# In-projection duals of a gated hybrid block: six accumulators in turning pairs, q stored whole, short conv in PSUM

## The chip, the cores and the metric

One core of a Trainium2 chip. The metric is the device time of one launch in microseconds (us), the median of several runs. TensorE (PE) multiplies, VectorE (DVE) does two-input elementwise work, ScalarE (ACT) copies and evaluates activations, GpSimd (POOL) does elementwise work on SBUF, and SyncE (SP) issues most of the loads. PE writes only into PSUM, which has eight banks of 128 x 512 float32. Each engine works through its own instructions in a fixed order; an instruction that waits holds all behind it on that engine.

## The reference

One trunk layer over 1024 positions and 1024 channels, in float32. The part that matters here is the combined input projection and what follows each of its columns:

```python
proj = jnp.einsum('bsd,de->bse', h, w_in[l])
b_s, c_s, v_s, v_c, gl_c, gate_br = jnp.split(proj, SPLITS[:-1], axis=-1)

y_a = b_s * causal_dwconv(c_s * v_s, conv_short_w[l])        # width 3
y_a = jnp.einsum('bsc,cd->bsd', y_a, w_short_out[l])

u = v_c * jax.nn.sigmoid(gl_c)
u = causal_dwconv(u, conv_conf_w[l]) + conv_conf_b[l]         # width 31
u = jax.nn.silu(layer_norm(u, conf_ln_g[l], conf_ln_b[l]))
y_b = jnp.einsum('bsc,cd->bsd', u, w_conf_out[l])

g_a, g_b = jnp.split(jax.nn.sigmoid(gate_br), 2, axis=-1)
mix = jnp.einsum('bsd,de->bse', g_a * y_a + g_b * y_b, w_o[l])
```

Ahead of it stand an adaptive RMSNorm and its modulation; behind it a gated feed-forward network and a last norm.

## The kernel before

Channels lie on the 128 partitions, so a block of 128 channels by 1024 positions is one tile, and `halves` are its two halves of 512 positions. Each float32 operand of a matmul is split into a high and a low part (`split_w` for weights, lines 201 to 211; `split` for data), and each product is three matmuls: high by high, high by low, low by high (`mm3`, lines 285, 286 and 288). For a weight, ACT casts the high part `wh` (line 207), then POOL or DVE subtracts it from `raw` for the low part `wl` (line 208).

After a lead of seven column blocks and one more, the other 48 column blocks of the projection are worked off as twelve **duals** (here dual 0 to dual 11, in the order of `PAIRS`, two pairs in each). A dual computes a 2 x 2 block product with seven products instead of eight. The names of the products are M1 to M7 and their order is `PRODUCTS = "1265734"`: M1, M2, M6, M5, M7, M3, M4. Each has two halves, p = 0 and 1, one for each pair of the dual, and a half is 12 matmuls of 512 columns. Before M6 POOL makes the sums of weight blocks (lines 230 to 232), and before M3 one more (line 234). A unit of weights is prepared two products ahead (`next_w`, `AHEAD`), from three buffers each of `wh` and `wl` and five of `raw`; the four loads of the next dual are asked for at M3.

Each half of a product accumulates in a bank: M1, M6, M7 and M4 one after another in x, M2 in y, M5 and M3 in z. `win_evac` takes the values out after each product: c11 = M1 + M2, c12 = M1 + M6 + M5 + M3, c22 = M1 + M6 + M7 + M5 and c21 = -(M1 + M6 + M7 + M4), the signs being folded into what follows. ACT copies x after M1 (line 579) and after M6, and z after M5 (line 594), into SBUF; `plus` (line 547) adds a bank to such a copy. What a pair is, its kind says:

- `p` (channels of c_s and v_s): their product (lines 587 and 608), then `short_conv` (ACT line 538, DVE line 540, over all 1024 positions in SBUF).
- `q` (two blocks of b_s): times the short conv `sc` of two blocks (lines 589, 600, 611), then `q_store` splits the result: an ACT cast and a POOL subtraction for each half (lines 531 and 532) into a `qs` tile of high and low, stored from SP (line 534). In the last dual `q_load` brings high and low back, four transfers a block.
- `u` (v_c and gl_c): the gated product (lines 585 and 606) into `u`.
- `g` (two gate blocks): sigmoids, stored to DRAM by ACT.

The tiles of p, sc, u, sig and qs all come from one pool `uc` of eight. The width-31 conv (`conv`) is DVE work between all this: for each u tile two differences and 46 taps (line 649) of 512 columns, whose accumulators stand in the two banks left, `ps2`. A tap is ordered behind an instruction of the list `reads`, which holds the DVE additions of M2, M7 and M3; `CONV_READS = 66` spreads the taps over the first 66 of 72. ACT finishes a block of conv with two activations with the bias (line 662), and POOL adds it to `tot` (line 669). After the duals comes `ya` (the short branch's output projection), which needs all of q split.

Of the kernel before, what the change touches and what calls it, by code (L numbers as in the profile page):

```python
# [39 lines left out]
P = 128  # L40
# [35 lines left out]
PAIRS = [  # L76
# [4 lines left out]
]  # L81


CONV_READS = 66

NORM_AT = 1
LAG = 2  # L90
# [19 lines left out]
def block_kernel(ctx: ExitStack, tc: tile.TileContext, x0, xT, c, vecs, ada, w_first, w_plain, w_duals,  # L110
# [66 lines left out]
    def col(base, k):  # L177
        return vec[:, base + k : base + k + 1]
# [234 lines left out]
    def uc_tile(name, n=T + CK - 1, dt=F32):  # L413
        return ucp.tile([P, T + CK - 1], dt, tag="uc", name=name)[:, :n]
# [111 lines left out]

    def q_store(j):

        for h in range(2):
            s = uc_tile("qs", T, F32R)  # L530
            nc.scalar.copy(s[:, :H], sc[j][:, halves[h]])
            nc.gpsimd.tensor_tensor(s[:, H:], sc[j][:, halves[h]], f32(s[:, :H]), ALU.subtract)
            q_dram[j, h] = dram.tile([P, T], F32, name=f"q{j}{h}")
            nc.sync.dma_start(q_dram[j, h], f32(s))

    def short_conv(j, p):
        sc[j] = uc_tile(f"sc{j}", T)
        nc.scalar.activation(sc[j], p[:, :T], AF.Copy, scale=col(V_SW, j))
        for s in range(1, SK):
            nc.vector.scalar_tensor_tensor(  # L540
                out=sc[j], in0=p[:, s : s + T], scalar=col(V_SW + s * KC, j), in1=sc[j], op0=ALU.mult, op1=ALU.add
            )

    reads = []

    def plus(out, ps, b):
        reads.append(nc.vector.tensor_tensor(out, ps, b, ALU.add).ins)

    def minus_times(out, a, b):

        nc.vector.scalar_tensor_tensor(out=out, in0=a, scalar=-1.0, in1=b, op0=ALU.mult, op1=ALU.mult)

    def win_evac(pairs):

        st = [{} for _ in pairs]

        def start(e, kind, j):
            if kind == "u":
                u.append(u_tile(j))
                e["b"] = [u[j][:, CK - 1 + h * H : CK - 1 + (h + 1) * H] for h in range(2)]  # L560
            elif kind == "p":
                e["p"] = uc_tile(f"p{j}", T + SK - 1)
                nc.vector.memset(e["p"][:, : SK - 1], 0.0)
                e["b"] = [e["p"][:, SK - 1 + h * H : SK - 1 + (h + 1) * H] for h in range(2)]
            elif kind == "g":
                e["t"] = [uc_tile("sig", T) for _ in range(2)]
                e["b"], e["c"] = ([t[:, s] for s in halves] for t in e["t"])

        def evac(i, m, ps):
            kind, j, *rest = pairs[i]  # L570
            e = st[i]
            if m == "1":
                start(e, kind, j)
                if kind == "q":
                    e["b"] = [g_tile("m")]
            if m == "6" and kind == "q":
                e["b"].append(g_tile("v"))
            if m in "16":
                nc.scalar.copy(e["b"][m == "6"], ps)
            elif m in "23":  # L580
                h = m == "3"
                b = e["b"][h]
                plus(b, ps, b)
                if kind == "u" and h:
                    nc.vector.tensor_tensor(b, b, e["z"], ALU.mult)
                elif kind == "p" and h:
                    minus_times(b, e["z"], b)
                elif kind == "q":
                    nc.vector.tensor_tensor(sc[j][:, halves[h]], b, sc[j][:, halves[h]], ALU.mult)
                elif kind == "g":  # L590
                    nc.scalar.activation(b, b, AF.Sigmoid)
            elif m == "5":
                e["z"] = e["c"][1] if kind == "g" else g_tile("z")
                nc.scalar.copy(e["z"], ps)
            elif m == "7":
                plus(e["z"], ps, e["z"])
                if kind in "ug":
                    nc.scalar.activation(e["z"], e["z"], AF.Sigmoid, scale=-1.0)
                elif kind == "q":
                    minus_times(sc[j + 1][:, halves[1]], e["z"], sc[j + 1][:, halves[1]])  # L600
            else:
                if kind in "ug":
                    sig = e["c"][0] if kind == "g" else g_tile("sig")
                    nc.scalar.activation(sig, ps, AF.Sigmoid, scale=-1.0)
                if kind == "u":
                    nc.vector.tensor_tensor(e["b"][0], e["b"][0], sig, ALU.mult)
                elif kind == "p":
                    minus_times(e["b"][0], ps, e["b"][0])
                    short_conv(j, e["p"])
                elif kind == "q":  # L610
                    minus_times(sc[j + 1][:, halves[0]], ps, sc[j + 1][:, halves[0]])
                    for i in range(2):
                        q_store(j + i)
                else:
                    for g, t in zip((j, *rest), e["t"]):
                        nc.scalar.dma_start(gate_dram[g], t)
        return evac

    qT = [[None, None] for _ in range(KC)]

    def q_load(j, h):
        qT[j][h] = t_pair(f"q{j}{h}")
        for t, s in zip(qT[j][h], halves):
            nc.sync.dma_start(f32(t), q_dram[j, h][:, s])
# [6 lines left out]
    NE = (T + CK - 1) // 2  # L631
    TAPS = CK // 2 * 3 + 2

    def conv(j):
        eo = u[j].rearrange("p (n two) -> p n two", two=2)
        ev, od = eo[:, :, 0], eo[:, :, 1]
        diff = diffp.tile([P, T + CK - 1], F32, tag="diff", name="diff")
        d, e = diff[:, :NE], diff[:, NE : 2 * NE - 1]
        with tc.issue_after(reads[j * CONV_READS // KC]):
            nc.vector.tensor_tensor(d, ev, od, ALU.subtract)  # L640
            nc.vector.tensor_tensor(e, ev[:, 1:], od[:, : NE - 1], ALU.subtract)
        a0, a1 = ps2_tile("c0"), ps2_tile("c1")
        n = 0

        def tap(out, src, s, wt, acc):
            nonlocal n
            n += 1
            with tc.issue_after(reads[(j * TAPS + n) * CONV_READS // (KC * TAPS)]):
                tap.ins = nc.vector.scalar_tensor_tensor(  # L649
                    out=out, in0=src[:, s : s + H], scalar=wt, in1=acc, op0=ALU.mult, op1=ALU.add  # L650
                ).ins

        nc.scalar.activation(a0, od[:, :H], AF.Copy, scale=wsum[:, j : j + 1])
        for s in range(1, CK // 2 + 1):
            last = s == CK // 2
            tap(a0, od, s, col(V_CW + 2 * s * KC, j) if last else wsum[:, s * KC + j : s * KC + j + 1], a0)
        for s in range(CK // 2):
            tap(a1, e, s, col(V_CW + (2 * s + 1) * KC, j), a1 if s else a0)
        for s in range(CK // 2 + 1):
            tap(a0, d, s, col(V_CW + 2 * s * KC, j), a0)  # L660
        for i, a in enumerate((a0, a1)):
            nc.scalar.activation(eo[:, : H, i], a, AF.Identity, bias=col(V_CB, j))
        nc.scalar.dma_start(cv_dram[j], u[j][:, :T])

    def add_conv(j):

        with tc.issue_after(pool_los[(j + 1) * CONV_READS * 7 // (6 * KC) + 5]):
            for h in range(2):
                nc.gpsimd.tensor_tensor(tot[h], tot[h], u[j][:, halves[h]], ALU.add)

# [34 lines left out]
        return [rstd_end(*r) for r in rs]  # L705

    n_duals = len(PAIRS) // 2
    for d in range(n_duals):
        banks, evac = {}, win_evac(PAIRS[2 * d : 2 * d + 2])
        for i, m in enumerate(PRODUCTS):  # L710
            product(banks, m, th[m], evac, y_tile=ps_tile)
            if d == n_duals - 1:
                for n in range(4 * i, min(4 * i + 4, 2 * KC)):
                    q_load(n // 2, n % 2)

    zs = {}

    def act_b(k, h):
# [467 lines left out]
```

## Time and profile before

| | us |
|---|---|
| median of three runs | 1514.88 |
| lowest, highest run | 1513.08, 1517.58 |
| span of the profiled execution | 1514.3 |
| first matmul of the duals, from the start of the span | 113.84 |
| first matmul of `ya` | 585.04 |
| PE busy | 1475.4 |
| DVE busy | 1173.1 |
| POOL busy | 580.2 |
| ACT busy | 613.6 |

A profile row of a group reads: line, engine, operation, output<-inputs, shapes, count | total busy us, mean ns of one | idle us of that engine right before them, with what ended it. A row of a timeline reads: start, duration, engine, line, operation, output<-inputs, shape, count, and in brackets how long the engine stood idle before it and what released it. A row of waits reads: who waited for whom, us in total, times, the longest. A busy PE is not PE at its peak, since matmuls overlap: in the profile one of 512 columns takes 0.39 us, while an undisturbed stretch starts one about every 0.227 us.

### The profile page before, as it was taken

To read this page: it belongs to the slowest core of one execution; us is meant where nothing else is said; L and a number is where in the kernel's file an instruction comes from. 1 tells how busy PE (TensorE), PEld (TensorE's weight loads), DVE (VectorE), ACT (ScalarE), POOL (GpSimd) and SP (SyncE) were. 2 spreads that over 40 slices of the span, in tenths; PEclk is the share of its full clock that TensorE was granted. 3 is DMA by queue.
4 is the path that set the end of the run, shared out by engine and by line. 5 is a ranking of instruction groups with operands and counts; after the bars stand their busy time and mean duration, and the time that the engine had idled before them with its cause. 6 is when DMAs were issued, how large, how long until landed. Compare 5 with 4: busy or idle time off the path is not lost.

```text
span 1514.3 us, 17807 instructions
## 1 busy us (share of the span) xinstructions
PE 1475.4 (97%) x6455; PEld 1203.2 (79%) x6455; DVE 1173.1 (77%) x1561; ACT 613.6 (41%) x875; POOL 580.2 (38%) x483
## 2 busy tenths in 40 slices
PE   6999999999998999999999989999999999999997
PEld 2788887877886888888788868888888888888887
DVE  7897898989998882857876798876666665767755
ACT  4654333333332442325335464444444443211235
POOL 0037788788768884320121101110000006444105
PEclk9999999999999999999999999999999999999999
DMA  9522224223222259655754527644444449997403
GB/s 347 206 64 84 84 71 139 70 98 111 98 84 85 69 192 408 239 197 173 249 193 155 167 89 231 209 153 153 153 153 153 153 150 363 348 330 241 152 28 112
DMA packets 87306, 255.64 MB, mean 169 GB/s; under 512 B 10033, under 2 KB 12209, under 8 KB 87218
## 3 DMA queue, kind: packets, MB, share of 16 engines
q1 hardware_dynamic: 46384, 146.30, 28.9%
q0 software_dynamic: 36944, 95.44, 19.0%
q10 hardware_dynamic: 3890, 12.78, 2.1%
q8 instruction: 50, 0.82, 0.2%
q14 instruction: 38, 0.31, 0.1%
HBM read 187.89 MB, written 66.58 MB: 168 GB/s over the span
## 4 chain that ended last, share of the span: by engine, by line
PE 78%; DVE 10%; POOL 7%; issue 3%; DMA 1%; ACT 1%; SPq 0%; POOLq 0%; ACTq 0%; DVEq 0%
PE x L288 10%; PE x L286 10%; PE x L285 10%; PE z L286 5%; PE z L285 5%; PE z L288 5%; DVE c L649 4%; PE y L288 3%; PE y L285 3%; PE y L286 3%; POOL wl L208 3%; PE ya L285 2%; PE mix L285 2%; PE mix L286 2%; PE ya L288 2%
## 5 line engine op out<-in xcount | busy, mean ns | idle before, releaser
L207 ACT CAST wh<-raw 128x1024 fp32r<-128x1024 f32 (+2 forms) x257 | 259.1, 1009 | 417.0 <-PE x L286 107.0
L208 POOL TENSOR_TENSOR wl<-raw,wh 128x1024 fp32r<-128x1024 f32 x92 | 237.0, 2584 | 87.6 <-ACT wh L207 81.1
L208 DVE TENSOR_TENSOR wl<-raw,wh 128x1024 fp32r<-128x1024 f32 (+2 forms) x165 | 188.1, 1141 | 50.8 <-ACT wh L207 48.4
L649 DVE SCALAR_TENSOR_TENSOR c<-diff,vec,c 128x512 f32<-128x512 f32 x248 | 182.2, 749 | 6.4 <-DMA q<-qs 2.6
L912 POOL DMA_DIRECT2D hid<-stage x71 | 37.9, 534 | 356.7 <-DVE stage L325 351.5
L285 PE MATMUL x<-th,wh 128*128 128x512 f32 x336 | 130.7, 389 | 0.0
L286 PE MATMUL x<-tl,wh 128*128 128x512 f32 x336 | 130.7, 389 | 0.0
L288 PE MATMUL x<-th,wl 128*128 128x512 f32 x336 | 130.7, 389 | 0.0
L649 DVE SCALAR_TENSOR_TENSOR c<-u,wsum,c 128x512 f32<-128x512 f32 x112 | 84.0, 750 | 2.0
L285 PE MATMUL x<-t2h,wh 128*128 128x512 f32 x184 | 73.6, 402 | 5.5 <-ACT wh L207 2.8
L288 PE MATMUL x<-t2h,wl 128*128 128x512 f32 x184 | 73.5, 400 | 4.5 <-POOL wl L208 4.2
L266 DVE CUSTOM_DVE_ANT_0 raw<-raw,cs,vec 128x1024 f32<-128x1024 f32 x24 | 36.9, 1541 | 48.9 <-DMA raw<-in_ada 39.7
L286 PE MATMUL x<-t2l,wh 128*128 128x512 f32 x184 | 73.4, 399 | 0.1
L286 PEld LDWEIGHTS x<-tl,wh 128*128 128x128 f32 x336 | 63.1, 188 | 13.2
L288 PEld LDWEIGHTS x<-th,wl 128*128 128x128 f32 x336 | 63.1, 188 | 13.1
L285 PEld LDWEIGHTS x<-th,wh 128*128 128x128 f32 x336 | 63.1, 188 | 13.0
L230 POOL TENSOR_TENSOR raw<-raw 128x1024 f32<-128x1024 f32 x12 | 29.2, 2437 | 99.1 <-DVE wl L208 95.3
L288 PE MATMUL z<-th,wl 128*128 128x512 f32 x168 | 65.5, 390 | 0.0
L285 PE MATMUL z<-th,wh 128*128 128x512 f32 x168 | 65.4, 389 | 0.0
L286 PE MATMUL z<-tl,wh 128*128 128x512 f32 x168 | 65.4, 389 | 0.0
L324 ACT CAST stage<-g 128x512 fp32r<-128x512 f32 x62 | 38.3, 621 | 54.6 <-DMA hid<-stage 26.8
L325 DVE TENSOR_TENSOR stage<-g,stage 128x512 fp32r<-128x512 f32 x62 | 42.4, 687 | 20.1 <-ACT stage L324 19.9
(802 smaller groups left out, 4076.5 us busy)
## 6 DMA issues: line engine op xcount, KB each, us to landing
hid<-stage POOLq DMA_DIRECT2D x71, 512.0 KB, 4.0
raw<-in_w_fi SPq DMA_DIRECT2D x50, 512.0 KB, 4.4
raw<-in_w_duals SPq DMA_DIRECT2D x48, 512.0 KB, 3.5
th<-hid POOLq DMA_DIRECT2D x71, 256.0 KB, 5.7
tl<-hid POOLq DMA_DIRECT2D x71, 256.0 KB, 5.8
ada<-in_ada SPq DMA_DIRECT2D x24, 512.0 KB, 6.4
raw<-in_ada SPq DMA_DIRECT2D x24, 512.0 KB, 4.5
raw<-in_w_fo SPq DMA_DIRECT2D x24, 384.0 KB, 5.8
```

The source lines that it names most:

```text
L207: nc.scalar.copy(wh, raw)
L208: lo = lo_engine.tensor_tensor(wl, raw, f32(wh), ALU.subtract)
L230: eng.tensor_tensor(a["s1"], a["21"], a["22"], ALU.add)
L266: nc.vector.tensor_tensor_reduce(out=raw, in0=raw, in1=cs, scale=1.0, scalar=col(V_ADA, b), op0=ALU.mult, op1=ALU.add, accum_out=modc(b),)
L285: nc.tensor.matmul(ps, wh, xh, start=first, stop=False, skip_group_check=again)
L286: nc.tensor.matmul(ps, wh, xl, start=False, stop=False, skip_group_check=again)
L288: mm3.ins = nc.tensor.matmul(ps, wl, xh, start=False, stop=last, skip_group_check=again).ins
L324: nc.scalar.copy(hi, src)
L325: nc.vector.tensor_tensor(lo, src, f32(hi), ALU.subtract)
L649: tap.ins = nc.vector.scalar_tensor_tensor(out=out, in0=src[:, s : s + H], scalar=wt, in1=acc, op0=ALU.mult, op1=ALU.add).ins
L912: nc.gpsimd.dma_start(hid_dram[key], s)
```

## The change

- Six PSUM tiles are taken once, as three pairs. Dual by dual they change places: the pair that was y becomes x, z becomes y, x becomes z.
- After M1, ACT copies x into y, and M2 accumulates on it there (its first matmul no longer starts a new sum). c11 then stands whole in y, and the addition after M2 goes; for `u` and `p` ACT copies y to SBUF, for `g` its sigmoid reads y, for `q` DVE multiplies from y.
- c12 is added up in z and c21 taken from x, and multiplies and sigmoids read these banks. The u sigmoid of c21 is written into x itself.
- The short conv accumulates in the two x banks by halves; its last tap writes `sc`.
- q is stored whole, one transfer a block, with no split. In the last dual, after its first four products, it is loaded whole, and ACT and DVE split it.
- `reads` holds the instructions after M7, M3 and M4, each with a place in units of a product; the taps are spread evenly over 11.2 duals by place.
- In `PAIRS`, u7 goes into dual 8 in place of p6, and dual 9 gets p6 and p7.

The core of the diff:

```diff
-    ("q", 4), ("p", 6), ("p", 7), ("u", 7), ("q", 6), ("g", ("a", 2), ("a", 3)),
+    ("q", 4), ("u", 7), ("p", 6), ("p", 7), ("q", 6), ("g", ("a", 2), ("a", 3)),
...
-CONV_READS = 66
+CONV_DUALS = 11.2
+AT_READS = {"7": 4.5, "3": 5.5, "4": 6.5}
...
     def q_store(j):
-        for h in range(2):
-            s = uc_tile("qs", T, F32R)
-            nc.scalar.copy(s[:, :H], sc[j][:, halves[h]])
-            nc.gpsimd.tensor_tensor(s[:, H:], sc[j][:, halves[h]], f32(s[:, :H]), ALU.subtract)
-            q_dram[j, h] = dram.tile([P, T], F32, name=f"q{j}{h}")
-            nc.sync.dma_start(q_dram[j, h], f32(s))
+        q_dram[j] = dram.tile([P, T], F32, name=f"q{j}")
+        nc.sync.dma_start(q_dram[j], sc[j])
+
+    def short_conv(j, p, banks):
+        sc[j] = uc_tile(f"sc{j}", T)
+        for h, bank in enumerate(banks):
+            nc.scalar.activation(bank, p[:, h * H : (h + 1) * H], AF.Copy, scale=col(V_SW, j))
+        for h, bank in enumerate(banks):
+            for s in range(1, SK):
+                nc.vector.scalar_tensor_tensor(
+                    out=sc[j][:, halves[h]] if s == SK - 1 else bank, in0=p[:, h * H + s : h * H + s + H],
+                    scalar=col(V_SW + s * KC, j), in1=bank, op0=ALU.mult, op1=ALU.add
+                )
...
+    def q_load(j):
+        t = uc_tile("q", T)
+        nc.sync.dma_start(t, q_dram[j])
+        for h in range(2):
+            qT[j][h] = split(t[:, halves[h]], hl_tile, f"q{j}{h}")
...
+    def win_dual(d, pairs, x, y, z):
...
+        def c22(p, e, kind, j, *more):
+            src = y[p] if kind == "q" else e["5"]
+            add = nc.vector.tensor_tensor(src, x[p], e["5"], ALU.add)
...
+        def c12(p, e, kind, j, *more):
+            add = nc.vector.tensor_tensor(z[p], z[p], e["6"], ALU.add)
...
+            if kind == "u":
+                return times(e["b"][1], z[p], e["z"])
...
+        def c21(p, e, kind, j, *more):
...
+            if kind == "u":
+                nc.scalar.activation(x[p], x[p], AF.Sigmoid, scale=-1.0)
+                return times(e["b"][0], x[p], e["b"][0])
...
+        banks = {"1": x, "6": x, "7": x, "4": x, "2": y, "5": z, "3": z}
+        for m in PRODUCTS:
+            w = next_w()
+            for p in range(2):
+                ps, e = banks[m][p], st[p]
+                for k in range(KH):
+                    c0 = (p * KH + k) * P
+                    mm3([ps], slice(c0, c0 + P), w, [th[m][k]], m in "15" and k == 0, k == KH - 1, m not in "15")
+                if m == "1":
+                    nc.scalar.copy(y[p], ps)
+                elif m in "65":
+                    e[m] = g_tile("v")
+                    nc.scalar.copy(e[m], ps)
+                else:
+                    done = {"2": c11, "7": c22, "3": c12, "4": c21}[m](p, e, *pairs[p])
+                    if done is not None:
+                        reads.append((7 * d + AT_READS[m] + 0.5 * p, done.ins))
+            if d == len(PAIRS) // 2 - 1 and m in "1265":
+                for j in range(2):
+                    q_load(2 * "1265".index(m) + j)
+        for e, (kind, j, *more) in zip(st, pairs):
+            if kind == "p":
+                short_conv(j, e["t"], x)
+            elif kind == "q":
+                for i in range(2):
+                    q_store(j + i)
...
+    def paced(n):
+        at = 7 * CONV_DUALS * n / (KC * TAPS)
+        return [ins for when, ins in reads if when <= max(at, reads[0][0])][-1]
...
+    banks = [[ps_tile(b) for _ in range(2)] for b in "xyz"]
     for d in range(n_duals):
-        banks, evac = {}, win_evac(PAIRS[2 * d : 2 * d + 2])
-        for i, m in enumerate(PRODUCTS):
-            product(banks, m, th[m], evac, y_tile=ps_tile)
+        win_dual(d, PAIRS[2 * d : 2 * d + 2], *banks)
+        banks.append(banks.pop(0))
```

More of the change, by code (lines that the diff above doesn't have):

```diff
@@ L527, in q_store @@
     def q_store(j):
-        for h in range(2):
-            s = uc_tile("qs", T, F32R)
-            nc.scalar.copy(s[:, :H], sc[j][:, halves[h]])
-            nc.gpsimd.tensor_tensor(s[:, H:], sc[j][:, halves[h]], f32(s[:, :H]), ALU.subtract)
-            q_dram[j, h] = dram.tile([P, T], F32, name=f"q{j}{h}")
-            nc.sync.dma_start(q_dram[j, h], f32(s))
[L536 to L553, printed above, removed]
-        st = [{} for _ in pairs]
-        def start(e, kind, j):
+        q_dram[j] = dram.tile([P, T], F32, name=f"q{j}")
[10 more added lines that the diff above has]
+                )
@@ new lines, in block_kernel, with minus_times, times, c11 @@
+    reads = []
+    def minus_times(out, a, b):
+        return nc.vector.scalar_tensor_tensor(out=out, in0=a, scalar=-1.0, in1=b, op0=ALU.mult, op1=ALU.mult)
+    def times(out, a, b):
+        return nc.vector.tensor_tensor(out, a, b, ALU.mult)
+    qT = [[None, None] for _ in range(KC)]
+    def q_load(j):
+        t = uc_tile("q", T)
+        nc.sync.dma_start(t, q_dram[j])
+        for h in range(2):
+            qT[j][h] = split(t[:, halves[h]], hl_tile, f"q{j}{h}")
+    def win_dual(d, pairs, x, y, z):
+        st = [{} for _ in pairs]
+        mul = any(kind == "q" for kind, *_ in pairs)
+        def c11(p, e, kind, j, *more):
+            if kind == "q":
+                times(sc[j][:, halves[0]], y[p], sc[j][:, halves[0]])
+                return
@@ L561, in start @@
             elif kind == "p":
[L562 to L565, printed above, removed]
+                e["t"] = uc_tile(f"p{j}", T + SK - 1)
+                nc.vector.memset(e["t"][:, : SK - 1], 0.0)
+                e["b"] = [e["t"][:, SK - 1 + h * H : SK - 1 + (h + 1) * H] for h in range(2)]
+            else:
@@ L566, in start @@
                 e["t"] = [uc_tile("sig", T) for _ in range(2)]
                 e["b"], e["c"] = ([t[:, s] for s in halves] for t in e["t"])
[L569 to L600, printed above, removed]
-            else:
[L602 to L613, printed above, removed]
-                else:
-                    for g, t in zip((j, *rest), e["t"]):
-                        nc.scalar.dma_start(gate_dram[g], t)
@@ L617, in win_evac @@
[L617 to L624, printed above, removed]
+            nc.scalar.activation(e["b"][0], y[p], AF.Sigmoid if kind == "g" else AF.Copy)
+        def c22(p, e, kind, j, *more):
+            src = y[p] if kind == "q" else e["5"]
+            add = nc.vector.tensor_tensor(src, x[p], e["5"], ALU.add)
+            if kind == "q":
+                return minus_times(sc[j + 1][:, halves[1]], src, sc[j + 1][:, halves[1]])
+            if kind == "p":
+                e["z"] = src
+            else:
+                e["z"] = e["c"][1] if kind == "g" else src
+                nc.scalar.activation(e["z"], src, AF.Sigmoid, scale=-1.0)
+            return add
@@ new lines, in c12 @@
+        def c12(p, e, kind, j, *more):
+            add = nc.vector.tensor_tensor(z[p], z[p], e["6"], ALU.add)
+            if kind == "q":
+                return times(sc[j][:, halves[1]], z[p], sc[j][:, halves[1]])
+            if kind == "u":
+                return times(e["b"][1], z[p], e["z"])
+            if kind == "p":
+                return minus_times(e["b"][1], z[p], e["z"])
+            nc.scalar.activation(e["b"][1], z[p], AF.Sigmoid)
+            return add
+        def c21(p, e, kind, j, *more):
+            if kind == "q":
+                return minus_times(sc[j + 1][:, halves[0]], x[p], sc[j + 1][:, halves[0]])
+            if kind == "p":
+                return minus_times(e["b"][0], x[p], e["b"][0])
+            if kind == "u":
+                nc.scalar.activation(x[p], x[p], AF.Sigmoid, scale=-1.0)
+                return times(e["b"][0], x[p], e["b"][0])
+            nc.scalar.activation(e["c"][0], x[p], AF.Sigmoid, scale=-1.0)
@@ L627, in block_kernel @@
+        for e, (kind, j, *more) in zip(st, pairs):
+            if kind == "p":
+                short_conv(j, e["t"], x)
+            elif kind == "q":
+                for i in range(2):
+                    q_store(j + i)
+            elif kind == "g":
+                for g, t in zip((j, *more), e["t"]):
+                    nc.scalar.dma_start(gate_dram[g], t)
     taps = vec[:, V_CW : V_CW + CK // 2 * 2 * KC].rearrange("p (j two k) -> p j two k", two=2, k=KC)
@@ L638, in conv @@
         d, e = diff[:, :NE], diff[:, NE : 2 * NE - 1]
-        with tc.issue_after(reads[j * CONV_READS // KC]):
+        with tc.issue_after(paced(j * TAPS)):
             nc.vector.tensor_tensor(d, ev, od, ALU.subtract)
@@ L647, in tap @@
             n += 1
-            with tc.issue_after(reads[(j * TAPS + n) * CONV_READS // (KC * TAPS)]):
+            with tc.issue_after(paced(j * TAPS + n)):
                 tap.ins = nc.vector.scalar_tensor_tensor(
@@ L665, in add_conv @@
     def add_conv(j):
-        with tc.issue_after(pool_los[(j + 1) * CONV_READS * 7 // (6 * KC) + 5]):
+        with tc.issue_after(pool_los[min(int(7 * CONV_DUALS * (j + 1) / KC) + 5, len(pool_los) - 1)]):
             for h in range(2):
```

3 lines of the change are left out of this document (removed).

## The prediction

> **What bounds the kernel now.** I began with the busy table and went straight to the stage that the change edits, the twelve duals, one window each.
>
> ```profile
> PE 1475.4 (97%) x6455; PEld 1203.2 (79%) x6455; DVE 1173.1 (77%) x1561; ACT 613.6 (41%) x875; POOL 580.2 (38%) x483
> ...
> 113.84:151.92 38.08, 38.08 (x169) 31.53 (x168) 29.46 (x39) 15.55 (x21) 28.39 (x15) 1.00 0.25 83
> 228.08:267.34 39.26, 38.88 (x170) 31.30 (x168) 33.70 (x53) 14.56 (x20) 33.70 (x18) 1.00 0.39 134
> 305.42:345.60 40.18, 38.71 (x170) 31.38 (x168) 36.41 (x44) 15.45 (x21) 36.23 (x16) 1.00 0.28 95
> 345.60:385.46 39.86, 38.41 (x169) 31.46 (x168) 37.96 (x55) 15.82 (x22) 34.88 (x17) 1.00 0.31 106
> 461.62:508.88 47.26, 41.66 (x169) 33.60 (x168) 37.90 (x54) 15.78 (x20) 40.61 (x18) 0.93 0.26 89
> 546.96:585.04 38.08, 38.08 (x169) 31.53 (x168) 17.44 (x25) 16.22 (x24) 25.09 (x13) 1.00 0.88 330
> 113.84:585.04 471.20, 462.30 (x2017) 379.99 (x2016) 412.44 (x530) 177.94 (x241) 376.87 (x165) 0.99 0.32 110
> ```
>
> Columns after the window: its length, then busy us (count) of PE, PEld, DVE, ACT, POOL, granted clock, DMA share, GB/s. A dual is 7 products x 2 halves x 12 matmuls = 168. Dual 0 shows it undisturbed: 38.08 us, so 5.44 a product and 2.72 a half. Twelve of them are 457.0 us; the stage takes 471.2. The change removes no matmul, so **all that it can win in this stage is 14.2 us**, and the windows say where it lies: dual 3 1.2, dual 5 2.1, dual 6 1.8, dual 9 9.2 (sum 14.3); the other eight are clean. DVE, busy 412 of 471 us, is no bound by itself. What the PE waited for in this stage:
>
> ```profile
> PE x L288 <- POOL wl L208: 7.4, 4, 2.8
> PE y L288 <- POOL wl L208: 1.2, 1, 1.2
> PE x L285 <- ACT u L579: 0.4, 1, 0.4
> ...
> 465.08 0.80 PE L288 MATMUL x<-h00h,wl 128*128 128x512 f32 x1 [2.84 <-POOL wl L208]
> 465.67 0.63 PE L285 MATMUL x<-h10h,wh 128*128 128x512 f32 x1
> 480.40 0.50 PE L288 MATMUL x<-t2h,wl 128*128 128x512 f32 x1 [2.76 <-POOL wl L208]
> ```
>
> It is the low half of a weight, made on POOL, five times. After the two longest the matmul takes 0.63 us, and dual 9 has clock 0.93: 7% of 47.26 is 3.3 us lost at half rate, 1.65 for each of the two. So 5.9 of waiting costs 9.2.
>
> Why is POOL late there? Its rows ahead of the late weights of duals 3, 6 and 9 (and ACT's row ahead of dual 9's first):
>
> ```profile
> 234.54 2.56 POOL L532 TENSOR_TENSOR qs<-sc,qs 128x512 fp32r<-128x512 f32 x2
> 237.06 2.40 POOL L208 TENSOR_TENSOR wl<-raw,wh 128x1024 fp32r<-128x1024 f32 x1
> ...
> 353.13 3.02 POOL L532 TENSOR_TENSOR qs<-sc,qs 128x512 fp32r<-128x512 f32 x2
> 356.11 4.75 POOL L208 TENSOR_TENSOR wl<-raw,wh 128x1024 fp32r<-128x1024 f32 x2
> ...
> 460.01 0.62 ACT L531 CAST qs<-sc 128x512 fp32r<-128x512 f32 x1 [6.98 <-DVE sc L589]
> 460.54 1.04 ACT L207 CAST wh<-raw 128x1024 fp32r<-128x1024 f32 x1
> ...
> 473.54 4.51 POOL L532 TENSOR_TENSOR qs<-sc,qs 128x512 fp32r<-128x512 f32 x2
> 478.00 4.71 POOL L208 TENSOR_TENSOR wl<-raw,wh 128x1024 fp32r<-128x1024 f32 x2
> ```
>
> All four are the q store of the dual before: POOL makes two `qs` tiles while the PE needs the weight queued behind them, and for dual 9's first weight ACT's high half `wh` stood behind a `qs` cast that waited 7 us for DVE. Duals 3, 6 and 9 are each the dual after a q dual.
>
> **The change, part by part.**
>
> *q whole via DRAM.* 16 casts and 16 POOL subtractions leave the stage:
>
> ```profile
> L532 POOL TENSOR_TENSOR qs<-sc,qs 128x512 fp32r<-128x512 f32 x16 | 23.5, 1480 | 7.1 <-ACT qs L531 7.1
> ```
>
> That frees 23.5 us of POOL and 9.9 of ACT (16 x 0.62). The stalls of duals 3, 6 and 9, 12.2 us, lose their cause. Next late are the three additions ahead of the third weight and `tot`, which stay; I credit 11.0. Bounds: 12.2, and 3.3 if dual 9, whose weights have also those additions before them, loses only a fifth of its 9.2 (1.8) and the others half of their 3.0 (1.5).
>
> ```profile
> q<-qs SPq DMA_DIRECT2D x16, 512.0 KB, 2.6
> ```
>
> On SP 16 stores become 8 of the same size, each still waiting for `sc`. The next dual's weights are asked for two products earlier, so they stand ahead of the stores as before: 0 (a store that is late holds only loads a dual away). In return the last dual loads q in 8 transfers instead of 32 and splits it: 16 ACT casts and 16 DVE subtractions. At the 0.62 of a `qs` cast and, since these too read two SBUF tiles beside POOL, at most POOL's 1.48 each, that is 10 us of ACT and up to 24 of DVE, in a window where ACT is busy 16.2 and DVE 17.4 of 38.1. The same dual holds four `sig` tiles, u7 and up to four q tiles in a pool of eight, so an ACT sigmoid, or a q load on SP with `w_short`'s weights behind it, may wait for a slot. I take 0; if that cover is gone, the split ends after the dual, at worst 17.4 + 24 - 38.1 = 3.3 us.
>
> *Results and short conv in PSUM.*
>
> ```profile
> L547 DVE TENSOR_TENSOR p<-y,p 128x512 f32<-128x512 f32 x8 | 5.5, 684 | 3.7 <-PE y L288 3.7
> L540 DVE SCALAR_TENSOR_TENSOR sc<-p,vec,sc 128x1024 f32<-128x1024 f32 x16 | 39.6, 2477 | 1.3 <-ACT sc L538 1.3
> L606 DVE TENSOR_TENSOR u<-u,sig 128x512 f32<-128x512 f32 x5 | 12.7, 2535 | 0.0
> L649 DVE SCALAR_TENSOR_TENSOR c<-diff,vec,c 128x512 f32<-128x512 f32 x248 | 182.2, 749 | 6.4 <-DMA q<-qs 2.6
> ```
>
> M2's 24 additions go (24 x 0.684 = 16.4). Short conv becomes 32 half taps with a PSUM operand, like the 0.749 tap: 24.0 instead of 39.6, 15.6 less. The u multiply reads one SBUF tile instead of two: 2.535 to about 0.69, 9.2 less. Some 41 us off DVE, hidden under PE, worth nothing by itself; it shortens ACT's waits for DVE, ahead of `wh`. Dual 5's 2.1 hung on those waits, not on q; I credit half, 1.0 (bounds 0 and 2.1). ACT gains 13 copies of y, 13 x 0.58 = 7.5 us, against those 9.9 lost.
>
> *M2 on a copy of M1.* This is the new wait. M2 is the product right after M1. Before, it had a bank of its own, and M1's copy to SBUF was due only at the third product, three halves (8.2 us) later. Now the copy must stand in y when M2 starts, **one half, 2.72 us, after M1's half ends**. Queued behind M2 is the whole PE. Ahead of the copy on ACT stand `wh`, short-conv copies that wait for DVE, and the conv's last activation. As a bound I replay the M1 copies where ACT ran them, the late ones:
>
> ```profile
> 234.94 0.59 ACT L579 COPY p<-x 128x512 f32<-128x512 f32 x1 [0.45 <-ACT sig L604]
> 241.83 0.57 ACT L579 COPY u<-x 128x512 f32<-128x512 f32 x1
> 272.86 0.59 ACT L579 COPY p<-x 128x512 f32<-128x512 f32 x1
> 311.83 0.59 ACT L579 COPY m<-x 128x512 f32<-128x512 f32 x1 [0.40 <-PE x L288]
> 352.17 0.57 ACT L579 COPY p<-x 128x512 f32<-128x512 f32 x1
> 517.94 0.57 ACT L579 COPY sig<-x 128x512 f32<-128x512 f32 x1
> 553.72 0.59 ACT L579 COPY sig<-x 128x512 f32<-128x512 f32 x1 [0.45 <-ACT sig L604]
> ```
>
> M2 starts 5.44 after its dual, its second half 8.16 after. Dual 3: halves at 233.52 and 236.24, copies ready at 235.53 and 242.40, late by 2.0 and 6.2. Dual 4: 0.7; dual 5 (0.6 later by its own stall): 1.0; dual 6: 1.7; dual 10's second half: 1.5; dual 11: 1.9. The worst of each dual sum to 13.0, almost the whole prize. But what held the worst goes away:
>
> ```profile
> 237.17 0.08 DVE L418 MEMSET u<- 128x30 f32 x1 [5.13 <-POOL qs L532]
> ...
> 241.22 0.72 ACT L662 ACTIVATE u<-c,vec 128x512 f32<-128x512 f32 x1 [5.70 <-DVE c L649]
> ```
>
> DVE stood 5.1 us because u's slot was a `qs` tile's; the conv ended late; ACT stood 5.7; the copy came behind it. Bounds 0 and 13.0; I take 1.7, what duals 4 and 5 show, whose waits are not q's.
>
> *Turning banks.* y becomes the next x, z the next y, x the next z. M1's copy needs the old z free: from M3's first half to that copy is five halves, 13.6 us, and DVE's addition and product there take 1.4. M5 needs the old x, where short conv now runs, six halves (16.3 us) after M4. One conv is about 3 us of DVE between conv taps; dual 9 now has two (p6, p7), 6 us with as many taps between, plus the ACT copies: near the limit. I take 0.8, bounds 0 and 4.
>
> *Taps by time.* No tap more or fewer; 0.
>
> **Sum** against this execution's span: 1514.3 - 11.0 - 1.0 + 1.7 + 0.8 = 1504.8. The runs' median, 1514.88, is 0.6 above the span, so **1505.4**.
>
> One rule of the Trainium skill speaks to the price of the new wait. "TensorE: Matmul & The Clock Gate", Part 1, has the clock halved after an idle activity window of about 3.4 us; the two waits here, 2.84 and 2.76 by the rows, were followed by half rate already, so the row decides. By the rule M2 waits of 2 us would cost just themselves; by the row each that nears 3 us costs 1.65 more.
>
> **Rivals.**
>
> *The copy decides (slower).* Place: ACT's queue at the turn of each dual.
>
> ```profile
> ACT u L662 <- DVE c L649: 44.4, 12, 6.8
> ACT sc L538 <- DVE p L551: 18.6, 7, 5.7
> ```
>
> 19 waits of 63 us in all. If a third of that, 21 us, lies before an M1 copy and two of the waits end in half rate (3.3), then 1514.3 - 12.0 + 24.3 + 0.6 = 1527. It outweighs the gain from 12.0 us on, 0.5 a half. For: 2.72 us of slack, short conv's copies issued ahead of M1's. Against: the largest share sits behind q and behind two-SBUF operations, both gone. Chance 0.25.
>
> *Given back (no change).* Dual 9 keeps its stall, since additions and `tot` still precede its weights: only the lower bound, 3.3, is won, and M2 waits of 2.5 (dual 3's first half and a bit) take most of it: 1514.3 - 3.3 + 2.5 + 0.6 = 1514.1. Chance 0.14.
>
> *Below 1500* would take waits outside the stage; the change touches none. Chance 0.04.
>
> **How the numbers follow.** The forecast has 0.57, with its own range 1500.7 (all 14.2 won) to 1510. No change means within 0.3%, 4.5 us. Faster 0.57 + 0.04 = 0.61, same 0.14, slower 0.25. The range runs from 1498 to 1524, which leaves out half of the slow rival and part of the last.
>
> **What would show it.** Right: no wait of PE on `wl` after duals 2, 5 and 8; `wl` on POOL without `qs`; dual windows of 38.1 to 39. Wrong: waits of PE's y matmuls on ACT's y copy that sum to over 3 us (over 12: the slow rival); z matmuls that wait for DVE `sc` in dual 10; a late split ahead of `ya`; windows of dual 9 still above 42. The stage as I forecast it takes 471.2 - 12.0 + 2.5 = 461.7 us.

## The result, and the profile after

| | before | after |
|---|---|---|
| median (lowest to highest, 4 runs each), us | 1516.2 (1513.1 to 1517.6) | 1504.8 (1503.0 to 1505.8) |
| ratio, with its 95% interval | | 0.9922 (0.9906 to 0.9938) |
| span of the profiled execution | 1514.3 | 1501.2 |
| the twelve duals, first matmul to the first of `ya` | 471.2 | 459.5 |

The forecast was 1505.4, with 461.7 for the duals. The busy table after, and windows of the whole stage, of dual 2 and of dual 10, the only two that are longer than 38.1 us (columns as before):

```profile
PE 1469.3 (98%) x6455; PEld 1202.0 (80%) x6455; DVE 1141.0 (76%) x1569; ACT 623.1 (42%) x896; POOL 538.2 (36%) x467
...
112.78:572.29 459.51, 457.88 (x2017) 378.27 (x2016) 382.64 (x542) 188.99 (x265) 336.56 (x150) 1.00 0.31 106
188.94:228.12 39.18, 38.39 (x169) 31.46 (x168) 37.91 (x59) 14.93 (x21) 29.51 (x14) 1.00 0.27 92
494.68:534.21 39.53, 38.69 (x169) 31.38 (x168) 38.28 (x56) 15.31 (x21) 29.60 (x15) 1.00 0.33 116
```

Of the 14.2 us above the 457.0 of unhindered matmuls, 2.5 are left: 1.1 in dual 2, 1.4 in dual 10, and the granted clock is full. Of the 13.1 us by which the spans differ, 11.7 lie in this stage, 1.1 ahead of it and 0.3 behind it. The waits of PE in this stage after:

```profile
PE z L283 <- ACT z L623: 0.8, 2, 0.6
PE x L283 <- ACT x L623: 0.8, 1, 0.8
```

None is for a weight. All are M2 (whose banks are called z or x by now) that waits for ACT's copy of M1, line 623. What held the copy, in ACT's timeline of dual 2, then of dual 10:

```profile
194.11 0.69 ACT L534 ACTIVATE y<-p,vec 128x512 f32<-128x512 f32 x1 [1.93 <-DVE u L549]
194.74 0.54 ACT L623 COPY x<-z 128x512 f32<-128x512 f32 x1
...
498.68 1.35 ACT L534 ACTIVATE x<-p,vec 128x512 f32<-128x512 f32 x2 [1.10 <-DVE p L546]
499.96 0.54 ACT L623 COPY z<-y 128x512 f32<-128x512 f32 x1
501.96 0.69 ACT L534 ACTIVATE x<-p,vec 128x512 f32<-128x512 f32 x1 [1.46 <-DVE sc L537]
...
503.54 0.57 ACT L623 COPY z<-y 128x512 f32<-128x512 f32 x1
```

Line 534 is ACT's copy for the short conv. It needs an x bank that DVE has still to read, ACT waits, and M1's copy stands behind it. In dual 10 the second conv's copy waits for the first conv to leave the bank.

The costs of single pieces, and the wait of ACT for a conv's end, which was 44.4 us:

```profile
L537 DVE SCALAR_TENSOR_TENSOR x<-p,vec,x 128x512 f32<-128x512 f32 x10 | 7.4, 752 | 1.0 <-ACT x L534 0.7
L549 DVE TENSOR_TENSOR u<-y,u 128x512 f32<-128x512 f32 x2 | 1.4, 686 | 0.2 <-ACT y L610 0.2
L315 DVE TENSOR_TENSOR q51l<-q,q51h 128x512 fp32r<-128x512 f32 x1 | 2.9, 2893 | 0.0
ACT u L684 <- DVE c L671: 5.7, 6, 1.6
```

A half tap of the short conv takes 0.752 us and the u multiply 0.69, as priced. A split of q, with both inputs in SBUF, takes up to 2.9, where the prediction had at most 1.48; the sixteen together take 18.5, within its 24. By the Trainium skill, "SBUF — State Buffer", Who interferes with whom, a DVE instruction with two SBUF inputs contends with a GpSimd one that reads SBUF for a port pair that is an exclusive lock, and one with at most one SBUF input, outside the modes that use two ports, does not contend; the 2.535 us before and 0.69 after of the same multiply agree.

### The profile page after: what moved, and what is told of

Its sections match the earlier page's. It is cut to its first block, busy times and chain, and to the rows that moved or that the text cites. A ratio compares the mean times of both kernels' runs of the same rounds, so it can differ in the third digit from the quotient of the medians.

```text
span 1501.2 us, 17711 instructions
## 1 busy us (share of the span) xinstructions
PE 1469.3 (98%) x6455; PEld 1202.0 (80%) x6455; DVE 1141.0 (76%) x1569; ACT 623.1 (42%) x896; POOL 538.2 (36%) x467
## 4 chain that ended last, share of the span: by engine, by line
PE 93%; DVE 4%; issue 1%; ACT 1%; DMA 1%; POOL 0%; POOLq 0%; ACTq 0%; DVEq 0%
PE x L286 11%; PE x L284 11%; PE x L283 10%; PE z L283 7%; PE z L284 7%; PE z L286 7%; PE y L284 6%; PE y L283 6%; PE y L286 6%; PE ya L284 2%; PE mix L286 2%; PE mix L284 2%; PE ya L283 2%; PE ya L286 2%; PE mix L283 2%; PE yb L283 2%
## 5 line engine op out<-in xcount | busy, mean ns | idle before, releaser
L206 POOL TENSOR_TENSOR wl<-raw,wh 128x1024 fp32r<-128x1024 f32 x92 | 227.2, 2471 | 131.1 <-ACT wh L205 130.9
L283 PE MATMUL x<-th,wh 128*128 128x512 f32 x240 | 93.4, 389 | 0.0
L284 PE MATMUL x<-tl,wh 128*128 128x512 f32 x240 | 93.4, 389 | 0.0
L286 PE MATMUL x<-th,wl 128*128 128x512 f32 x240 | 93.4, 389 | 0.0
L956 POOL DMA_DIRECT2D th<-hid x71 | 38.1, 537 | 52.0 <-PE x L286 28.3
L283 PE MATMUL yb<-zsh,wh 128*128 128x512 f32 x128 | 50.0, 391 | 2.8 <-DVE gb L793 2.8
L283 PE MATMUL x<-t2h,wh 128*128 128x512 f32 x120 | 47.7, 400 | 5.1 <-ACT wh L205 2.8
L286 PEld LDWEIGHTS x<-th,wl 128*128 128x128 f32 x240 | 45.1, 188 | 9.4
L283 PEld LDWEIGHTS x<-th,wh 128*128 128x128 f32 x240 | 45.1, 188 | 9.3
L284 PEld LDWEIGHTS x<-tl,wh 128*128 128x128 f32 x240 | 45.1, 188 | 9.3
```

The source lines that it names most:

```text
L206: lo = lo_engine.tensor_tensor(wl, raw, f32(wh), ALU.subtract)
L283: nc.tensor.matmul(ps, wh, xh, start=first, stop=False, skip_group_check=again)
L284: nc.tensor.matmul(ps, wh, xl, start=False, stop=False, skip_group_check=again)
L286: mm3.ins = nc.tensor.matmul(ps, wl, xh, start=False, stop=last, skip_group_check=again).ins
L956: nc.gpsimd.dma_start(t, hid_dram[key][:, s])
```

## The experiments

Each was read by the length of its dual stage, since the rest of the program moves by up to 4.8 us between the profiles (1041.5 to 1046.2). The fences give the window of the whole stage (length, then busy us of PE, PEld, DVE, ACT, POOL) and single waits.

**q alone (e1).** The kernel before, with the whole store and the split at loading:

```diff
     def q_store(j):
-        for h in range(2):
...
-            q_dram[j, h] = dram.tile([P, T], F32, name=f"q{j}{h}")
-            nc.sync.dma_start(q_dram[j, h], f32(s))
+        q_dram[j] = dram.tile([P, T], F32, name=f"q{j}")
+        nc.sync.dma_start(q_dram[j], sc[j])
```

> The kernel before, with q alone changed: stored whole, loaded whole in the last dual and split there by ACT and DVE. Theory (the POOL subtractions and ACT casts of the q store made the weights late): the waits of duals 3, 6 and 9 go, dual 5's 2.1 us stays; the stage of the twelve duals (471.2 us before, 459.5 after, 457.0 without any wait) comes to 459 to 462 and the time to 1504 to 1507. Rival (the gain came from results and short conv in PSUM, which free DVE and the SBUF port that POOL needs): the stage stays at 468 or more, the time at 1512 or more.

1510.7 us, ratio 0.9961 (0.9948 to 0.9975). The stage, its dual 9 and its dual 11, then waits:

```profile
113.71:580.24 466.53, 460.85 (x2017) 380.50 (x2016) 437.87 (x548) 176.80 (x241) 358.14 (x149) 0.99 0.30 101
456.46:499.89 43.43, 39.99 (x169) 32.61 (x168) 38.46 (x55) 14.64 (x18) 37.44 (x15) 0.96 0.25 83
538.02:580.24 42.22, 39.98 (x169) 32.61 (x168) 39.45 (x45) 22.37 (x37) 22.75 (x10) 0.96 0.76 280
...
ACT u L659 <- DVE c L646: 54.2, 13, 8.5
...
445.39 0.74 ACT L659 ACTIVATE u<-c,vec 128x512 f32<-128x512 f32 x1 [7.18 <-DVE c L646]
446.00 1.05 ACT L207 CAST wh<-raw 128x1024 fp32r<-128x1024 f32 x1
...
447.12 2.41 POOL L208 TENSOR_TENSOR wl<-raw,wh 128x1024 fp32r<-128x1024 f32 x1 [7.04 <-ACT wh L207]
```

Between the two theories, and nearer to the rival's 468 and 1512. The waits of duals 3, 5 and 6 and the second one of dual 9 went. Dual 9's first did not: it is 5.35 us with its clock dip. Here no cast of q stands in ACT's queue; a weight's cast stands behind the end of a conv for which ACT waits 7.2 us, POOL idles 7.0, and from then on it works without a break until dual 9's first low half is done, at 460.45. The kernel before has the same chain there, and no q in it:

```profile
449.95 0.73 ACT L662 ACTIVATE u<-c,vec 128x512 f32<-128x512 f32 x1 [6.12 <-DVE c L649]
...
451.68 2.40 POOL L208 TENSOR_TENSOR wl<-raw,wh 128x1024 fp32r<-128x1024 f32 x1 [5.10 <-ACT wh L207]
...
455.75 2.39 POOL L230 TENSOR_TENSOR raw<-raw 128x1024 f32<-128x1024 f32 x1
...
459.37 2.89 POOL L231 TENSOR_TENSOR raw<-raw 128x1024 f32<-128x1024 f32 x1
462.22 2.81 POOL L208 TENSOR_TENSOR wl<-raw,wh 128x1024 fp32r<-128x1024 f32 x1
```

Left out between POOL's rows are two additions to `tot`. POOL is busy from 451.68 to 465.03, and PE starts on the low half at 465.08. The `wh` behind the `qs` cast at 460.01 was ready at 461.58, before POOL was free, so that cast did not hold up this low half.

And the split of q costs 4.1 us in dual 11, 2.24 of waiting and most of the rest at half rate. In e1 DVE is still at conv taps 16 us into this dual and makes its first split at 554.78; after the change it does so at 538.27, 4 us in. DVE's timeline near the end, and POOL's row beside it:

```profile
562.41 2.67 DVE L317 TENSOR_TENSOR q31l<-q,q31h 128x512 fp32r<-128x512 f32 x1
...
567.25 1.77 DVE L317 TENSOR_TENSOR q40l<-q,q40h 128x512 fp32r<-128x512 f32 x1
568.94 2.87 DVE L317 TENSOR_TENSOR q41l<-q,q41h 128x512 fp32r<-128x512 f32 x1
571.73 0.68 DVE L317 TENSOR_TENSOR q50l<-q,q50h 128x512 fp32r<-128x512 f32 x1
572.33 0.68 DVE L543 TENSOR_TENSOR sig<-x,sig 128x512 f32<-128x512 f32 x1
...
568.43 2.83 POOL L208 TENSOR_TENSOR wl<-raw,wh 128x1024 fp32r<-128x1024 f32 x1
```

The gate's addition at 572.33, which frees an x bank for M4, comes behind splits that take 1.8 to 2.9 us. So the split did not end after the dual, as the prediction feared: it stood ahead of a result that PE needed.

**The changed kernel with the old way of q (e2).** The reverse edit.

> The changed kernel with the old way of q: cast on ACT, subtraction on POOL, two stores a block, high and low loaded straight. Theory: the duals after a q dual wait for their weights again; with DVE 41 us lighter the casts come sooner, so perhaps half of the 12.2 us: stage 464 to 472, time 1509 to 1517. Rival (PSUM is what counts): stage under 461.5, time within 2 us of 1504.8.

1512.6 us, ratio 0.9971 (0.9961 to 0.9982). The stage, dual 3, the wait, and ACT and DVE there:

```profile
113.10:581.59 468.49, 461.12 (x2017) 379.94 (x2016) 362.96 (x522) 187.43 (x262) 352.73 (x165) 0.99 0.32 111
228.45:275.43 46.98, 41.26 (x170) 33.33 (x169) 36.48 (x54) 17.76 (x26) 33.74 (x18) 0.93 0.32 116
...
PE y L283 <- ACT y L625: 5.7, 2, 3.8
...
232.90 0.62 ACT L529 CAST qs<-sc 128x512 fp32r<-128x512 f32 x1 [1.69 <-POOL qs L530]
...
240.61 0.72 ACT L687 ACTIVATE u<-c,vec 128x512 f32<-128x512 f32 x1 [4.65 <-DVE c L674]
...
242.14 0.59 ACT L625 COPY y<-x 128x512 f32<-128x512 f32 x1
...
238.53 0.08 DVE L416 MEMSET u<- 128x30 f32 x1 [2.18 <-POOL qs L530]
```

9.0 us are back, within the range of the theory, but not as waits for weights: 8.9 of them are dual 3's, where M2 waits twice for the copy. The first wait, 1.95 us, stands behind ACT's `qs` casts; the second, 3.77, behind a conv's end, where DVE had waited for a slot that a `qs` tile held. It is the chain that the replay of the M1 copies had shown. The longer wait is followed by half rate, and the dual's clock drops to 0.93.

**M2 on the copy alone (e7).** The kernel before, and M2 accumulates on ACT's copy:

```diff
+            if seed and m == "1":
+                banks["y", p] = y_tile("y")
+                nc.scalar.copy(banks["y", p], ps)
...
-                plus(b, ps, b)
+                if h:
+                    plus(b, ps, b)
+                elif kind == "g":
+                    nc.scalar.activation(b, ps, AF.Sigmoid)
+                    reads.append(reads[-1])
+                else:
+                    reads.append(nc.vector.tensor_copy(b, ps).ins)
```

> The kernel before, with M2 alone accumulating on ACT's copy of M1 in y; after M2 a copy (for a gate its sigmoid) takes the place of the addition. Theory: with q's casts and the long DVE operations still on the way, ACT is late for the copy; the 14.2 us of old waits stay and 3 to 13 us of y matmuls waiting for ACT's copy come on top: stage 474 to 484, time 1518 to 1529. Rival (the copy is never late, since the order of ACT is planned anew): stage 471 or less, no wait of PE on the copy over 1 us in sum.

1529.6 us, ratio 1.0082 (1.0065 to 1.0099):

```profile
112.72:596.33 483.61, 465.43 (x2018) 381.82 (x2016) 412.57 (x523) 178.55 (x241) 374.32 (x165) 0.99 0.31 108
...
PE y L285 <- ACT y L311: 11.3, 6, 4.2
PE x L288 <- POOL wl L208: 6.7, 2, 4.0
```

12.4 us more in the stage, at the top of the expected range, and a time just above it. The replay gave 13.0, and its duals are the right ones: M2 waits 6.3 us in dual 3 (replayed 6.2), 0.9 in dual 4 (0.7), 1.6 in dual 6 (1.7), 1.4 in dual 10 (1.5) and 1.2 in dual 11 (1.9), but not at all in dual 5 (1.0). That makes 11.3. The 12.4 come out otherwise: half rate adds some 3 in dual 3 and dual 9 grows by 1.2, while the old waits of duals 3, 5 and 6, 5.1 in all, go. On the old kernel the copy does decide, as the slower rival has it.

**The short conv behind M1's copy (e4, e8).** First only written later in the program (e4), then ordered behind the copy (e8):

```diff
                 if m == "1":
-                    nc.scalar.copy(y[p], ps)
+                    copied = nc.scalar.copy(y[p], ps)
+                    if convs:
+                        with tc.issue_after(copied.ins):
+                            short_conv(*convs.pop(0))
```

> The changed kernel with the short conv of a dual written after the M1 copies of the next one, so that ACT's copies for it stand behind them. Theory (the 2.45 us left in duals 2 and 10 are M1's copy behind short conv copies that wait for DVE): these go, stage 457.0 to 457.6, time 1501.5 to 1504; M5 of the next dual has 16 us for the conv's banks and does not wait. Rival (the conv then ends too late for M5, which needs its banks): z matmuls wait, stage 460 or more.

> The changed kernel with ACT's copies for the short conv ordered behind M1's copy of the next dual (the first conv behind the first half's, a second behind the second half's). Writing it later in the program alone changed nothing: the same 2.45 us, with ACT's instructions in the same order. Theory: now the waits in duals 2 and 10 go, stage 457.0 to 458, time 1502 to 1504. Rival (the conv ends too late for M5, or DVE waits for it): new waits on z or elsewhere, stage 459.5 or more.

e4: 1504.0 us, ratio 0.9916 (0.9903 to 0.9930); e8: 1502.5 us, ratio 0.9903 (0.9888 to 0.9918). The stage of e4, then of e8:

```profile
113.59:573.13 459.54, 457.84 (x2017) 378.15 (x2016) 383.60 (x542) 189.21 (x265) 337.02 (x150) 1.00 0.31 106
```

```profile
112.64:569.60 456.96, 456.96 (x2018) 378.68 (x2016) 385.31 (x542) 187.03 (x262) 334.30 (x149) 1.00 0.31 105
```

e4 fits neither of its theories: the order on ACT stayed what it was. e8 has no wait left in the stage; the 2.5 us were short-conv copies ahead of M1's, and the conv still leaves its banks in time for M5.

**M2 in a sum of its own (e3).** In the changed kernel, M1 goes to SBUF and DVE adds M2, as before:

```diff
-                if m == "1":
-                    nc.scalar.copy(y[p], ps)
+                if m == "1":
+                    start(e, *pairs[p])
+                    nc.scalar.copy(e["b"][0], ps)
...
+            b = e["b"][0]
+            nc.vector.tensor_tensor(b, y[p], b, ALU.add)
```

> The changed kernel with M2 in a sum of its own, as before: ACT copies M1 to SBUF, DVE adds M2 to it. Theory (M2 on the copy is the change's price, 2.45 us, and its 16 us of DVE additions saved are hidden): the y matmuls wait no more, stage 457.0 to 458.5, time 1502 to 1504.5. Rival (without the additions DVE and ACT run ahead, so they are worth more than the waits): stage 461 or more.

1500.8 us, ratio 0.9889 (0.9872 to 0.9905), the lowest ratio of all, though its interval overlaps those of e4, e5 and e8:

```profile
112.74:569.70 456.96, 456.96 (x2017) 378.69 (x2016) 399.49 (x566) 182.04 (x251) 335.72 (x150) 1.00 0.30 104
ACT u L691 <- DVE c L678: 16.4, 8, 4.6
```

DVE is 17 us busier than after the change, ACT waits more for a conv's end, and no matmul waits. The stage is e8's to the hundredth: accumulating M2 on the copy costs 2.5 us with ACT's order as it is, nothing with e8's, and in neither does it gain.

**What cured dual 9 (e5, e6, e9, e10, e11).** From the changed kernel: the taps by count (e5), the short conv in SBUF (e6). From q alone: the taps by time (e9), the order of pairs (e10), results in PSUM (e11).

```diff
 # e5
-        at = 7 * CONV_DUALS * n / (KC * TAPS)
-        return [ins for when, ins in reads if when <= max(at, reads[0][0])][-1]
+        return reads[n * (len(reads) * 66 // 72) // (KC * TAPS)][1]
 # e6
+        nc.scalar.activation(sc[j], p[:, :T], AF.Copy, scale=col(V_SW, j))
+        for s in range(1, SK):
+            nc.vector.scalar_tensor_tensor(
+                out=sc[j], in0=p[:, s : s + T], scalar=col(V_SW + s * KC, j), in1=sc[j], op0=ALU.mult, op1=ALU.add
+            )
 # e9: the change's paced() with
+AT_READS = {"2": 2.0, "7": 4.5, "3": 5.5}
 # e10: the change's PAIRS
 # e11: e3 with the edits of e5 and e6 and the old PAIRS
```

> The changed kernel with the conv taps spread by count over the list of results (over 66/72 of it, as before), not by time. The q store alone left dual 9's first weight late (5.35 us), behind ACT's wait of 7 us for the end of a conv on DVE. Theory (that wait goes because DVE's operations left SBUF and run as long as planned): stage 459 to 461.5, time within 2 us of 1504.8. Rival (it goes because the taps are spread by time): waits of 3 us or more behind a conv's end, stage 463 or more.

> The changed kernel with the short conv in SBUF over all 1024 positions, as before. DVE gets back about 16 us of two-SBUF work, and the x banks are free after M4. Theory (relief of DVE is what cured dual 9): ACT waits for DVE grow again, M1's copies come later, stage 461 to 467, time 1506 to 1512. Rival (relief is hidden; the conv in the x banks only delays ACT): stage under 459.5, the waits of duals 2 and 10 gone.

> The kernel before with q whole and, besides, the conv taps spread by time over 11.2 duals. With q whole alone the stage kept 9.5 us of waits: dual 9's first weight 5.35 (ACT waits 7 us for a conv's end, the weight's cast behind it) and 4.15 in dual 11. If the spread by time is a cure of its own, dual 9's wait goes: stage 457 to 463. If not, as the changed kernel with taps by count already says (no such wait came back), it stays: stage 465 to 469.

> The kernel before with q whole and the new order of pairs (u7 in dual 8, p6 and p7 together in dual 9). If the order cures dual 9 (no p beside a q in dual 8, so fewer two-SBUF operations ahead of it): stage 458 to 463. If not: 465 to 469.

> The kernel before with q whole and results taken from PSUM (M2 in its own sum, short conv in SBUF, taps by count, the old order of pairs). If operands in PSUM are the cure, since DVE then waits for no port that POOL holds and ends a conv as planned: no wait in dual 9, stage 457 to 461, time 1501 to 1506. If not: 465 to 469.

The times: e5 1501.9 us, 0.9898 (0.9884 to 0.9913); e6 1507.0, 0.9932 (0.9918 to 0.9947); e9 1514.0, 0.9983 (0.9972 to 0.9994); e10 1513.9, 0.9984 (0.9974 to 0.9993); e11 1507.0, 0.9937 (0.9922 to 0.9952). The stages, and ACT's waits for a conv's end, of e5, e6, e9 (with its dual 9), e10 and e11 in turn:

```profile
113.74:571.19 457.45, 457.25 (x2017) 378.58 (x2016) 389.81 (x542) 187.84 (x262) 335.66 (x149) 1.00 0.31 105
ACT u L683 <- DVE c L670: 13.3, 7, 3.8
```

```profile
112.90:572.92 460.02, 457.93 (x2018) 378.34 (x2016) 398.43 (x526) 186.31 (x255) 344.20 (x149) 1.00 0.31 105
ACT u L681 <- DVE c L668: 22.3, 12, 4.0
```

```profile
113.42:583.99 470.57, 462.05 (x2018) 380.19 (x2016) 443.06 (x548) 176.09 (x241) 355.82 (x149) 0.99 0.30 100
460.09:498.17 38.08, 38.08 (x170) 31.53 (x168) 36.80 (x47) 13.88 (x18) 30.62 (x13) 1.00 0.25 83
ACT u L665 <- DVE c L652: 62.7, 15, 9.2
```

```profile
113.81:581.88 468.07, 459.99 (x2017) 379.46 (x2016) 436.92 (x545) 175.67 (x240) 358.87 (x149) 0.99 0.30 100
ACT u L659 <- DVE c L646: 59.8, 14, 10.3
```

```profile
112.62:575.25 462.63, 459.15 (x2017) 379.38 (x2016) 416.36 (x550) 179.68 (x243) 350.37 (x150) 1.00 0.31 103
ACT u L687 <- DVE c L674: 28.2, 11, 7.4
```

Four of these five fell outside what was expected. e5's stage is below its theory's 459 to 461.5; e6's lies between its two, 0.5 us above the changed kernel's, and its time cannot be told from it; e9's is above both of its ranges; e11 has no wait in dual 9, but its stage and time are above 461 and 1506. Only e10 came as one of its two cases had it.

Compare the third busy figure, DVE's, with the length of the stage. Among the kernels with q whole and M2 in its own sum, 437 to 443 us of DVE go with 466.5 to 470.6, 416 with 462.6, 399 with 457.0. Neither the spread by time nor the order of pairs shortens the stage of q alone. The spread by time does take dual 9's wait away (e9), but it brings 3.9 us each in duals 6 and 10 and 5.8 in dual 11; the order of pairs leaves dual 9 at 45.38. Results in PSUM take dual 9's wait away too and leave 5.7 us in duals 10 and 11 (e11). With the conv in PSUM as well nothing waits (e3), but e3 differs from e11 in its order and its spread too. By time, e9 and e10 gain less than e1's 0.9961, so their part in the change is no gain on that base; on the changed kernel the taps by count (e5) were 2.1 us shorter in the stage than those by time, since M1's copy was late only once.

Why dual 9's first wait goes is not settled. The conv that held ACT in dual 8 ends no earlier elsewhere: its last activations start 27.0 us into the dual in e1, 26.9 in e5 and in e11. What differs is ACT's order. In e5 and e11 the cast of the weight for M4 comes 5 us before them, in e1 behind them. e11 and e5 take their taps from another list of results than e1, behind M7, M3 and M4 and not behind M2, M7 and M3, and no run changes the list alone. So it may be the places of the taps that cure dual 9, and not DVE's shorter operations.

## Why the prediction was right, and where it was not

*The ceiling.* Right. The stage could win 14.2 us and no more; e3 and e8 reach 456.96, the forecast's 457.0.

*The sum.* Right in size: 11.7 won in the stage where it had 9.5 (12.0 less 2.5). The old waits went whole, 14.2 where it credited 12.0. That the new costs, 1.7 + 0.8, came to 2.5 is luck, since they arose in other duals and for another reason. So is the distance of only 0.6 us from the forecast time: before's median in the same set of runs is 1516.2, 1.35 above the one that the forecast started from, and the time won is 11.4 where it had 9.5.

*Why the weights were late.* Half wrong, and this is the weakest step of the prediction: "All four are the q store of the dual before". For duals 3 and 6 and dual 9's second wait it holds, e1 has none of them (though dual 3's row with a wait was for ACT's copy of M1, behind the conv that a `qs` tile had made late, and not for a weight). For dual 9's first it doesn't. The row showed ACT's `qs` cast waiting 7 us for DVE, and the cast was taken for the cause. By the rows of the old trace shown with e1, POOL was late because it had idled 5.1 us for a `wh` behind a conv's end, 10 us earlier. With q's casts gone that chain stayed, with ACT's wait at 7.2 us where it had been 6.1, and what it costs PE, waiting and half rate, grew from about 4.5 (2.84 and 1.65) to 5.35 us. Of the 11.0 credited to q, q alone won 4.7 in the stage (471.2 to 466.5): 9.7 of old waits gone, 0.8 more in dual 9, 4.1 new in dual 11.

*DVE's 41 us.* "Hidden under PE, worth nothing by itself" is too strong, though they are hidden under PE on average. q whole alone is worth 0.39%, the whole change 0.78%, and in the kernels compared above a busier DVE goes, roughly, with a longer stage. In dual 11 of e1 the trace shows how: a late DVE has the split of q ahead of a result that PE waits for. For dual 9 it is argued only, as said above. And with M2 on the copy and the other edits in place, the 16 us of the short conv (e6) are worth 0.5 us in the stage.

*The last dual.* Costed at 0, with 3.3 if its cover were gone. The cover is DVE's relief: after the change dual 11 has no wait, in e1 it has 4.1, a little over the bound, and not behind the dual but within it. The two other kernels with results in PSUM and the short conv still in SBUF have 4.6 (e11) and 1.9 (e6) there.

*Dual 5.* Credited half of 2.1; all of it went, and already with q alone, so it did hang on the old way of q and not on the additions after M2.

*The new wait.* Right in kind and size, wrong in place. The bound of 13.0 by replay stands beside 11.3 of M2 waits in e7, and the guess that the worst of it was q's stands beside e2, where 9.0 come back with q. What is left comes from the short-conv copies of ACT, named in the slower rival. The two convs of dual 9 did cost, 1.4 us, but by ACT's queue; no z matmul waited for DVE in dual 10.

*The rivals.* "The copy decides" holds on the old kernel (e7, 1529.6 us) and needs a DVE or a q store that is late; that it had forecast 1527, for another kernel, is near by chance. "Given back" rested on dual 9 keeping its stall: with q alone it keeps the first half of it, at 1510.7 us.

*The clock.* The Trainium skill's page "TensorE: Matmul & The Clock Gate", Part 1, ties half rate to a window of about 3.4 us without work. The runs put the edge lower, near 2 us. In the dual stages of all the traces here, every wait of 2.24 us or more was followed by matmuls that take 0.63 us, and none of 1.95 or less was; of the two between, 2.01 in e9 was and 2.09 in e7 was not. Half rate cost about 1.5 to 2.8 us each time. So the prediction's 1.65 for a wait near 3 us was fair, and after the change, where no wait reaches 1 us, the clock in the stage is 1.00.

## What to carry to other kernels

When a late instruction stands behind others on its engine, follow that engine back to where it last stood idle, and ask what ended that: an instruction that waited for long nearby need not be on the chain, as the `qs` cast was not. Before an accumulation is moved onto another engine's copy, replay when those copies ran in the old trace against their new due times; it gave each dual's wait to within 1 us here, though neither the half rate that followed nor the old waits that went, and it showed that the edit needs others beside it. Time taken off an engine that is 88% busy (412 of 471 us) can be worth a wait on the bound engine although it is no bound itself; then ask whether each edit of the bundle still pays, as one of these did not.

## What was not expected of the hardware

The same subtraction on DVE, two SBUF inputs of 128 x 512, took 0.68 us and 2.87 us within 3 us of each other in dual 11 of e1. The long one ran from 568.94 to 571.81 beside a POOL subtraction that ran from 568.43 to 571.26; the short one followed while POOL stood idle. A busy share counts such stretches as work, so part of e1's 437.9 us of DVE is such time.
